# A two-layer decoder on one core: pair 10 of both feed-forward layers by half-size products, halves of the down projection one pair later, the next pair's first remainders ahead of evictions, and 23 warming matmuls

## The chip, the core and the metric

The kernel runs on one core of one Trainium2 chip. The metric is the device time of one execution in microseconds; three runs of the kernel before are shown, with their median.

## The reference, cut to what matters

The program is a decoder trunk with one RG-LRU layer and one RWKV-7 layer, each followed by a gated convolutional feed-forward layer. There are 512 tokens, a width of 1024 and a hidden width of 3072, all in float32. The change lies in the feed-forward layers and in the very first instructions.

```
def _conv_ffn(x, norm, w_up, conv_w, conv_b, w_down):
    h = _rmsnorm(x, norm)
    u = jnp.einsum('btd,df->btf', h, w_up)
    gate = _causal_dwconv(u[..., :D_FF], conv_w, conv_b)
    hid = jax.nn.gelu(gate, approximate=True) * u[..., D_FF:]
    return jnp.einsum('btf,fd->btd', hid, w_down)
```

## The kernel before

Every float32 operand is split into a high part, rounded by a cast, and a low part, the remainder (hi and lo; wh and wl for weights that go through `split`). A product is three matmuls: high by high, high by low, low by high (`mm3`, L77; all its matmuls are recorded at L81). ScalarE (ACT) casts the high parts, VectorE (DVE) subtracts for the low parts. An instruction that waits for the remainder therefore waits for a chain of a load, a cast and a subtraction.

**A feed-forward layer** (`ffn`, L580) treats the 3072 gate columns and the 3072 up columns in 12 pairs of 256 columns each, numbered 0 to 11. A pair's work on TensorE (PE) has one of two forms.

- `Whole` (L696) has four products G0, U0, G1, U1: each is half of the contraction for the gate or the up columns, 24 matmuls of 128x128 by 128x512.
- `Halves` (L725) writes the pair's product as seven half-size products in the manner of Strassen and Winograd, numbered 1 to 7 and made in the order 1, 2, 6, 5, 7 and then 3, 4. Each has 24 matmuls of 128x128 by 128x256. They accumulate into the banks A, D, A, F, A, F, A. `HALVES` says which pairs have this form: 3 to 9 and 11.

For each half-size product, `Halves.weights` makes the weights: some are blocks of the weights as loaded, some are sums of two (on DVE, L736, or by an accumulating transfer on GpSimd's queue, L753 and L206). Then a cast on ACT makes hi and a subtraction on DVE makes lo (both L743). hi1 and lo1 are those of product 1, and so on.

`Halves.product` runs a product and then evicts its bank: ACT copies bank A for products 1, 6 and 7 (L770, tile s); DVE adds bank D to s for 2 (L775), bank F for 7 and 3 (L780, L783), and writes the gate rows gpad (L781, L787). After product 4, `gate` (L681) runs the causal convolution (first tap on ACT, L687; two more on DVE, L689; tile cv) and the gelu on ACT (L690, tile ge), once for each of the pair's two blocks. Then two halves s of the up columns are multiplied by ge (L792, each by both blocks' gelus), cast to the high part of hid on ACT (L793), and the low part is subtracted on DVE (L794).

**The down projection** (`down`, L837) takes hid of two pairs (four blocks of 128) into one half of the output columns: 48 matmuls in two pieces, c0 and c1. The function `between` runs between the pieces: there products 3 and 4 of the current pair are made. So on PE one steady pair runs 1, 2, 6, 5, 7, c0, 3, 4, c1, and then the next pair's 1. The accumulators are added to the residual x on DVE (L871) in the first layer; in the second they go to xtok (L862). The last eight blocks (pairs 8 to 11) are a final projection in two groups of output columns.

**Order.** A tile scheduler keeps, on each engine, an order of its own making; `behind` adds an edge between two instructions for the order alone. The weights are loaded by SyncE's queue in the order of a plan (`plan_weights`, L135), which `gu` and `dd` write: `gu(n)` the blocks of a pair, `dd` those of a down half. `weights_load` and `weights_split` run ahead of use by counts; `cap` and `ahead` limit how far the next pair's weights are made. Raw, high and low blocks of weights share 24 buffers of 0.5 MB.

**The start.** While the first loads are on their way, 17 transposes of the identity run on PE (`WARM`, L382), before the first projection of the RG-LRU layer (L251, then L81).

Of the kernel before, what the change touches and what calls it, by code (L numbers as in the profile page):

```python
# [10 lines left out]
ALU = mybir.AluOpType  # L11
# [14 lines left out]
GN_EPS = 64e-5  # L26
DECAY_C = 0.6065306597126334
N4 = 24
WARM = 17

HALVES = (3, 4, 5, 6, 7, 8, 9, 11)

PARAMS = [
    [("lru_b_in", 16), ("lru_conv_w", 32), ("lru_conv_b", 8),
# [37 lines left out]
class Kernel:  # L72
# [62 lines left out]
    def plan_weights(self):  # L135
# [17 lines left out]
        def ffn(l):  # L153
            up, dn = ("ffn_w_up", (l,)), ("ffn_w_down", (l,))

            def gu(n):
                self.quads[l, n] = len(plan)
                a = lambda i, j: piece(up, j * 512, (1 - i) * DFF + n * 256, 4)
                if n in HALVES:
                    for first, more in (((1, 1), (1, 0)), ((0, 0), None), ((0, 1), None), ((1, 0), (0, 0)), ((1, 1), None)):  # L160
                        plan.append((a(*first), 4, True, more and a(*more)))
                else:
                    for i, j in ((1, 0), (0, 0), (1, 1), (0, 1)):
                        plan.append((a(i, j), 4, False, None))

            def dd(row, n, groups):
                for g in groups:
                    for k in range(0, n, 2):
                        add(dn, row + k * P, g * 512)

            for n in range(12):
                gu(n)
                if 2 <= n < 10:
                    dd((n // 2 - 1) * 512, 4, (n % 2,))
            dd(2048, 8, (0, 1))

        full(("lru_w_in", (0,)), [2, 3, 0, 1])
# [402 lines left out]
    def ffn(self, l, xs, finish, after=None):  # L580
        nc, tc = self.nc, self.tc
        last = l == 1
        with tc.tile_pool(name=f"ffn{l}", bufs=1) as pool:
# [38 lines left out]
            H = T // 2  # L622
# [34 lines left out]
            def behind(ins, prev):  # L657
                tc.add_manual_dep(ins.ins, prev.ins.name, NOSYNC, reason="order")

            def hidden(n):  # L660

                if last and n // 2 % 2:
                    if n == 2:
                        self.drain()
                    if n % 2 == 0:
# [59 lines left out]
            class Halves(Pair):  # L725
# [29 lines left out]
                def product(pair, p):  # L755
# [24 lines left out]
                        tt(s[7], s[7], bank["F"], ALU.add)  # L780
                        stt(gp[:, :, 2 + H :], s[7], -1.0, rb(H, T), ALU.mult, ALU.mult)  # L781
                    if p == 3:
                        tt(s[6], s[6], bank["F"], ALU.add)  # L783
                        if not last:
                            tt(s[6], s[6], rb(H, T), ALU.mult)
                    if p == 4:
                        stt(gp[:, :, 2 : 2 + H], bank["A"], -1.0, rb(0, H), ALU.mult, ALU.mult)  # L787
                        for e in range(2):
                            pair.gate(e)
                        pair.room()  # L790
                        for x, h in ((s[1], lo), (s[6], hi)):
                            tt(x, x, pair.ge[:, :, h], ALU.mult)  # L792
                            nc.scalar.copy(pair.hid[:, :, 0, h], x)  # L793
                            tt(pair.hid[:, :, 1, h], x, pair.hid[:, :, 0, h].bitcast(F32), ALU.subtract)  # L794
# [16 lines left out]
            def products(upto, more=2):  # L811

                while True:
# [1 line left out]
                    at[0] += 1  # L815
                    ahead(at[0] + more)
                    pairs[n].product(p)
                    if p == "G0" and n == 10:
                        self.weights_load(quads[n + 1] + 4)
                    if p == "G1" and n == 2:  # L820
                        self.weights_load(quads[n + 1] + 2)
                    if n == 0 and p in ("G0", "U0"):
                        start(int(p == "U0"))
                    if n == 1 and p == "U0":
# [12 lines left out]
            def down(g, b0, blocks, between=None):  # L837
# [29 lines left out]
                else:  # L867
# [8 lines left out]
                        if between and c == 0:  # L876
                            between()

                    self.project(hids, ev, kb=blocks, join=1 if between else 2, rate=0.5 if final else 2, after=hook, x0=b0)

            rooms = []

# [5 lines left out]
            cap[0] = seq.index((2, "U1")) + 1  # L888
            products((2, "U1"))
            cap[0] = len(seq)  # L890

            def between():
                self.weights_load(quads[3] + 4)
                ahead(at[0] + 1)

            down(0, 0, 4, between)
            ahead(at[0] + 2)
            for n in (*range(3, 10), 11):
                if n == 11:
                    products((10, "U1"))  # L900
                cap[0] = seq.index((n, 7)) + 1
                products((n, 7))
                cap[0] = seq.index((n, 4)) + 1
                ahead(at[0] + 2)
                following = n + 1 in HALVES
                if following:
                    self.weights_load(quads[n + 1] + 2)

                def between():
                    products((n, 3))  # L910
                    cap[0] = len(seq)
                    if following:
                        self.weights_load(quads[n + 1] + 4)
                    products((n, 4))
                    if following:
# [931 lines left out]
```

## Time and profile before

| | us |
|---|---|
| median of three runs | 1282.51 |
| lowest and highest run | 1281.61, 1282.84 |
| the profiled execution, its time | 1282.94 |
| the profiled execution, its span on the core | 1281.2 |
| TensorE busy in the span | 1248.3 |
| VectorE busy | 963.6 |
| ScalarE busy | 654.9 |
| GpSimd busy | 124.0 |

The profiled execution is one run, recorded by the hardware; its time is a little longer than its span, as the work around the first and last instruction belongs to it. The mean granted clock of TensorE in it is 0.994 of full. The page's groups name line, engine, operation and tiles, with the number of instructions, busy time and mean duration. A timeline gives the start in us from the span's start, the duration, and in brackets the idle time before an instruction and what ended it. The chain of waits goes back from the last instruction to what released it, step by step.

### The profile page before, as it was taken

How to read it: one execution, taken by the hardware profiler on the slowest of the kernel's cores; microseconds unless marked ns; L12 is line 12 of the kernel's file. 1: busy time of each engine (PE TensorE's matmuls, PEld its weight loads, DVE VectorE, ACT ScalarE, POOL GpSimd, SP SyncE). 2: the span in 40 equal slices, each digit the busy share in tenths (PEclk: the TensorE clock that was granted, in tenths of full speed). 3: DMA queues.
4: the chain of work that ended last, by engine and by line, in shares of the span. 5: the costliest groups of instructions: out<-in, count | busy, mean ns of one | idle time of the engine just before them, and what ended most of it. 6: DMA issues, size and time to landing. Idle time of an engine off the chain costs nothing.

```text
span 1281.2 us, 23259 instructions
## 1 busy us (share of the span) xinstructions
PE 1248.3 (97%) x9645; PEld 1076.6 (84%) x9645; DVE 963.6 (75%) x1451; ACT 654.9 (51%) x1013; POOL 124.0 (10%) x204
## 2 busy tenths in 40 slices
PE   9999999999999999999999999999999999999997
PEld 7777888999999988877678888778889999999886
DVE  6988688477777777789999877778863767777764
ACT  6697454344444444459845356545742444444442
POOL 0000000000000000010002244410000000000000
PEclk9999999999999999999999999999999999999999
DMA  6322234566666642423203112123345666665431
GB/s 255 99 66 83 92 106 115 148 166 171 174 165 165 197 104 82 140 58 126 82 18 107 44 54 84 61 84 99 117 92 147 168 168 165 164 167 190 105 116 66
DMA packets 46506, 154.08 MB, mean 120 GB/s; under 512 B 5984, under 2 KB 8288, under 8 KB 46272
## 3 DMA queue, kind: packets, MB, share of 16 engines
q1 hardware_dynamic: 38480, 125.32, 30.0%
q0 software_dynamic: 7056, 25.69, 11.6%
q8 instruction: 76, 1.25, 0.4%
q10 hardware_dynamic: 864, 1.57, 0.4%
q14 instruction: 30, 0.25, 0.1%
HBM read 148.05 MB, written 4.52 MB: 119 GB/s over the span
## 4 chain that ended last, share of the span: by engine, by line
PE 35%; DVE 12%; ACT 3%; issue 2%; POOL 1%; POOLq 0%; DVEq 0%; ACTq 0%
PE accA L81 5%; PE acc L81 4%; PE accF L81 4%; PE accU L81 3%; PE accG L81 3%; PE acc L857 3%; PE acc L859 3%; PE acc L858 3%; DVE X L1346 1%; DVE lo L743 1%; DVE wl L127 1%; PE accD L81 1%; DVE DA L1344 1%; DVE cv L689 1%; PE s L1460 1%
## 5 line engine op out<-in xcount | busy, mean ns | idle before, releaser
L127 DVE TENSOR_TENSOR wl<-raw,wh 128x1024 fp32r<-128x1024 f32 (+1 forms) x137 | 164.8, 1213 | 26.0 <-ACT wh L123 24.8
L743 DVE TENSOR_TENSOR lo<-raw,hi 128x1024 fp32r<-128x1024 f32 x112 | 134.7, 1219 | 15.5 <-ACT hi L743 15.4
L123 ACT CAST wh<-raw 128x1024 fp32r<-128x1024 f32 (+1 forms) x136 | 139.2, 1044 | 8.8 <-DMA raw<-in_weights_dram 5.0
L743 ACT CAST hi<-raw 128x1024 fp32r<-128x1024 f32 x112 | 113.5, 1050 | 40.4 <-DVE raw L736 19.3
L81 PE MATMUL accA<-xt,hi 128*128 128x256 f32 x768 | 133.9, 277 | 0.0
L81 PE MATMUL acc<-hid,wh 128*128 128x512 f32 x384 | 118.4, 393 | 1.9 <-ACT wh L123 1.9
L81 PEld LDWEIGHTS accA<-xt,hi 128*128 128x128 f32 x768 | 116.2, 188 | 0.0
L81 PE MATMUL accA<-xt,lo 128*128 128x256 f32 x384 | 106.3, 277 | 0.0
L770 ACT COPY s<-accA 128x512 f32<-128x512 f32 x48 | 28.1, 585 | 136.5 <-PE accA L81 136.5
L687 ACT ACTIVATE cv<-gpad,pv 128x512 f32<-128x512 f32 x48 | 37.5, 812 | 110.3 <-DVE gpad L787 97.5
L81 PEld LDWEIGHTS acc<-hid,wh 128*128 128x128 f32 x384 | 71.3, 190 | 16.2 <-ACT wh L123 2.4
L81 PE MATMUL accU<-xs,wh 128*128 128x512 f32 x256 | 79.5, 392 | 0.0
L81 PE MATMUL accG<-xs,wh 128*128 128x512 f32 x256 | 79.5, 392 | 0.0
L81 PE MATMUL acc<-xs,wh 128*128 128x512 f32 x248 | 77.8, 394 | 0.0
L857 PE MATMUL acc<-wh,hid 128*128 128x512 f32 (+1 forms) x200 | 76.8, 384 | 0.0
L858 PE MATMUL acc<-wh,hid 128*128 128x512 f32 (+1 forms) x200 | 76.8, 384 | 0.0
L859 PE MATMUL acc<-wl,hid 128*128 128x512 f32 (+1 forms) x200 | 76.7, 384 | 0.0
L81 PE MATMUL acc<-hid,wl 128*128 128x512 f32 x192 | 74.2, 394 | 0.0
L689 DVE SCALAR_TENSOR_TENSOR cv<-gpad,pv,cv 128x512 f32<-128x512 f32 x96 | 67.7, 746 | 7.4 <-ACT cv L687 7.3
L81 PEld LDWEIGHTS accA<-xt,lo 128*128 128x128 f32 x384 | 72.2, 188 | 0.0
L206 POOL DMA_DIRECT2D raw<-in_weights_dram x32 | 28.3, 884 | 358.0 <-DVE s L780 131.5
L81 PE MATMUL acc<-mix,wh 128*128 128x512 f32 x192 | 60.6, 399 | 2.2 <-ACT wh L123 2.2
(379 smaller groups left out, 3156.0 us busy)
## 6 DMA issues: line engine op xcount, KB each, us to landing
raw<-in_weights_dram SPq DMA_DIRECT2D x215, 512.0 KB, 3.7
raw<-in_weights_dram POOLq DMA_DIRECT2D x48, 512.0 KB, 5.6
xd<-x SPq DMA_DIRECT2D x8, 256.0 KB, 2.2
AR<-xd SPq DMA_DIRECT2D x1, 2048.0 KB, 9.3
x<-in_xT_dram SPq DMA_DIRECT2D x3, 512.0 KB, 6.9
out_dram<-xtok ACTq DMA_DIRECT2D x4, 256.0 KB, 2.1
out_dram<-xtok SPq DMA_DIRECT2D x4, 256.0 KB, 2.0
raw<-in_weights_dram SPq DMA_DIRECT2D x2, 256.0 KB, 4.9
```

The costliest lines, as they stand in the source:

```text
L81: mm = lambda *a, **kw: self.nc.tensor.matmul(ps, *a, skip_group_check=more, **kw)
L123: put = (self.nc.vector.tensor_copy if dve else self.nc.scalar.copy)(hi, src)
L127: rest = self.nc.vector.tensor_tensor(lo, src, hi.bitcast(F32), ALU.subtract)
L206: self.nc.gpsimd.dma_start(raw, more, accum_op=ALU.add)
L687: nc.scalar.activation(cv, pair.gp[:, e, 0:T], AF.Identity, bias=self.vec(f"ffn_conv_b{l}", fb), scale=cw(0))
L689: nc.vector.scalar_tensor_tensor(cv, pair.gp[:, e, j : j + T], cw(j), cv, ALU.mult, ALU.add)
L743: pair.at[p] = nc.scalar.copy(hi, f[p]), tt(lo, f[p], hi.bitcast(F32), ALU.subtract)
L770: copied = nc.scalar.copy(s[p], bank["A"])
L857: nc.tensor.matmul(ps, hh[:, s], wh[:, k, m], start=kk == 0, stop=False)
L858: nc.tensor.matmul(ps, hl[:, s], wh[:, k, m], start=False, stop=False)
L859: nc.tensor.matmul(ps, hh[:, s], wl[:, k, m], start=False, stop=kk == blocks - 1)
L1344: nc.vector.tensor_tensor(w, A[:, s + 1 :, s : s + 1].to_broadcast([P, n, j]), X[:, s : s + 1, 0:j].to_broadcast([P, n, j]), ALU.mult)
```

## The change

1. `WARM` is 23 and not 17.
2. `HALVES` is 3 to 11 without a gap: pair 10 is made by half-size products too, in both layers.
3. The down halves come one pair later. Before, the halves of pairs 0 and 1 were run after pairs 2 and 3 and so on to pair 9; now after pairs 3 and 4 and so on to pair 10. The plan of loads moves with them. The second layer's tile for hid of pairs 2 and 3 of each four is allocated once.
4. `later` adds two edges: the next pair's low part of product 1 stands ahead of the eviction of product 3 (L783, now L786), and that of product 2 ahead of the eviction of product 4 (L787, now L790). `cap` is lifted before product 3 and not after it, so these weights are made in time for the edges.
5. The final projection of the first layer splits weights three pieces ahead and not two.

Below L660 the lines of the changed kernel are 3 more at first (L783 is L786), and 1 more in `down` (L871 is L872).

```diff
-WARM = 17
+WARM = 23
-HALVES = (3, 4, 5, 6, 7, 8, 9, 11)
+HALVES = range(3, 12)
...
-                if 2 <= n < 10:
-                    dd((n // 2 - 1) * 512, 4, (n % 2,))
+                if 3 <= n < 11:
+                    dd((n - 3) // 2 * 512, 4, ((n - 3) % 2,))
...
+            def later(ins, n, p):
+                if n in pairs and p in pairs[n].at:
+                    behind(ins, pairs[n].at[p][1])
...
                     if p == 3:
-                        tt(s[6], s[6], bank["F"], ALU.add)
+                        later(tt(s[6], s[6], bank["F"], ALU.add), pair.n + 1, 1)
...
                     if p == 4:
-                        stt(gp[:, :, 2 : 2 + H], bank["A"], -1.0, rb(0, H), ALU.mult, ALU.mult)
+                        later(stt(gp[:, :, 2 : 2 + H], bank["A"], -1.0, rb(0, H), ALU.mult, ALU.mult), pair.n + 1, 2)
...
-                    if p == "G0" and n == 10:
+                    if p == "G0" and n == 2:
                         self.weights_load(quads[n + 1] + 4)
-                    if p == "G1" and n == 2:
-                        self.weights_load(quads[n + 1] + 2)
...
-                    self.project(hids, ev, kb=blocks, join=1 if between else 2, rate=0.5 if final else 2, after=hook, x0=b0)
+                    self.project(hids, ev, kb=blocks, join=1 if between else 2, rate=0.5 if final else 2, after=hook, x0=b0, ahead=3 if final else 2)
...
-            for n in (*range(3, 10), 11):
-                if n == 11:
-                    products((10, "U1"))
+            for n in range(3, 12):
                 cap[0] = seq.index((n, 7)) + 1
                 products((n, 7))
                 cap[0] = seq.index((n, 4)) + 1
                 ahead(at[0] + 2)
...
                 def between():
-                    products((n, 3))
                     cap[0] = len(seq)
-                    if following:
+                    if n < 11:
                         self.weights_load(quads[n + 1] + 4)
                     products((n, 4))
...
                 if n < 11:
-                    down(n % 2, (n // 2 - 1) * 4, 4, between)
+                    down((n - 3) % 2, (n - 3) // 2 * 4, 4, between)
```

How the instructions stand now is shown at three places. Buffer numbers are kept in the names.

**VectorE, first layer, from one steady pair's end into the next pair.** lo1 and lo2 are the next pair's remainders of products 1 and 2, gpad the eviction of product 4, cv the convolution, s the up columns. Before:

```order
L783 TENSOR_TENSOR s_3003<-s_3003,accF_3005 128x512
L785 TENSOR_TENSOR s_3003<-s_3003,rb_1450 128x512
L787 SCALAR_TENSOR_TENSOR gpad0_1364<-accA_2915,rb_1450 128x2x256
L743 TENSOR_TENSOR lo1_3143<-raw67_3081,hi1_3142 128x1024
L743 TENSOR_TENSOR lo2_3147<-raw68_3137,hi2_3146 128x1024
L689 SCALAR_TENSOR_TENSOR cv_3176<-gpad0_1364,pv_79,cv_3176 128x512
L689 SCALAR_TENSOR_TENSOR cv_3181<-gpad0_1364,pv_79,cv_3181 128x512
...
L736 TENSOR_TENSOR raw67_3081<-raw66_3078,raw67_3081 128x1024
L792 TENSOR_TENSOR s_2940<-s_2940,ge_3175 128x512
L792 TENSOR_TENSOR s_3003<-s_3003,ge_3175 128x512
L743 TENSOR_TENSOR lo6_3195<-raw67_3081,hi6_3194 128x1024
```

After, in the same place:

```order
L746 TENSOR_TENSOR lo1_3055<-raw65_3019,hi1_3054 128x1024
L786 TENSOR_TENSOR s_2941<-s_2941,accF_2943 128x512
L746 TENSOR_TENSOR lo2_3085<-raw66_3049,hi2_3084 128x1024
L788 TENSOR_TENSOR s_2941<-s_2941,rb_1456 128x512
L790 SCALAR_TENSOR_TENSOR gpad0_1370<-accA_2853,rb_1456 128x2x256
L739 TENSOR_TENSOR raw65_3019<-raw64_3016,raw65_3019 128x1024
L692 SCALAR_TENSOR_TENSOR cv_3114<-gpad0_1370,pv_79,cv_3114 128x512
L692 SCALAR_TENSOR_TENSOR cv_3119<-gpad0_1370,pv_79,cv_3119 128x512
...
L746 TENSOR_TENSOR lo6_3133<-raw65_3019,hi6_3132 128x1024
L795 TENSOR_TENSOR s_2878<-s_2878,ge_3113 128x512
L795 TENSOR_TENSOR s_2941<-s_2941,ge_3113 128x512
```

lo1 and lo2 stood behind gpad and now stand ahead of the evictions of products 3 and 4; the sum of weights (raw65) now comes before the convolution and lo6 before the multiplications of s by ge.

**ScalarE, first layer, at the same place.** ge are the two gelus, COPY of accA the eviction of product 1 of the next pair, hi6 and hi5 casts of its weights. Before:

```order
L687 ACTIVATE cv_3176<-gpad0_1364,pv_79 128x512
L687 ACTIVATE cv_3181<-gpad0_1364,pv_79 128x512
L690 ACTIVATE ge_3175<-cv_3176 128x512
L690 ACTIVATE ge_3175<-cv_3181 128x512
L743 CAST hi6_3194<-raw67_3081 128x1024
L793 CAST hid_3186<-s_2940 128x2x256
L793 CAST hid_3186<-s_3003 128x2x256
L770 COPY s_3252<-accA_3227 128x512
L743 CAST hi5_3254<-raw66_3078 128x1024
```

After:

```order
L690 ACTIVATE cv_3114<-gpad0_1370,pv_79 128x512
L690 ACTIVATE cv_3119<-gpad0_1370,pv_79 128x512
L746 CAST hi6_3132<-raw65_3019 128x1024
L693 ACTIVATE ge_3113<-cv_3114 128x512
L773 COPY s_3190<-accA_3165 128x512
L693 ACTIVATE ge_3113<-cv_3119 128x512
L746 CAST hi5_3192<-raw64_3016 128x1024
L796 CAST hid_3124<-s_2878 128x2x256
L796 CAST hid_3124<-s_2941 128x2x256
L773 COPY s_3253<-accA_3165 128x512
```

The cast hi6 and the copy of accA (product 1) now stand ahead of the second gelu, and hi5 ahead of the casts of hid. Seven of the eight transitions from one halved pair to the next in the first layer have this order.

**ScalarE, second layer, at the same place of a steady pair, after:**

```order
L690 ACTIVATE cv_10942<-gpad1_9475,pv_79 128x512
L690 ACTIVATE cv_10947<-gpad1_9475,pv_79 128x512
L746 CAST hi6_10960<-raw171_10848 128x1024
L693 ACTIVATE ge_10941<-cv_10942 128x512
L746 CAST hi5_11020<-raw170_10845 128x1024
L693 ACTIVATE ge_10941<-cv_10947 128x512
L773 COPY s_11018<-accA_10993 128x512
L796 CAST hid_10952<-s_10708 128x2x256
L796 CAST hid_10952<-s_10770 128x2x256
```

Here hi6 and hi5 stand ahead of a gelu each, and the copy stands behind both gelus; before, both layers had the order that the first of ScalarE's pieces above shows.

More of the change, by code (lines that the diff above doesn't have):

```diff
@@ L664, in hidden @@
                         self.drain()
-                    if n % 2 == 0:
                         self.xhid = self.const.tile([P, 2, 2, 2, T], F32R, tag="x", name="hid", bufs=1)
@@ L886, in room @@
                 return rooms[-1][:, b % 2, 0], rooms[-1][:, b % 2, 1]
-            cap[0] = seq.index((2, "U1")) + 1
             products((2, "U1"))
[L890 to L897, printed above, removed]
-            for n in (*range(3, 10), 11):
-                if n == 11:
-                    products((10, "U1"))
+            for n in range(3, 12):
                 cap[0] = seq.index((n, 7)) + 1
@@ L904, in ffn @@
                 ahead(at[0] + 2)
-                following = n + 1 in HALVES
-                if following:
+                if n < 11:
                     self.weights_load(quads[n + 1] + 2)
                 def between():
-                    products((n, 3))
                     cap[0] = len(seq)
-                    if following:
+                    if n < 11:
                         self.weights_load(quads[n + 1] + 4)
                     products((n, 4))
-                    if following:
+                    if n < 11:
                         ahead(at[0] + 3)
```

## Prediction

> **What bounds the kernel now.** I read the page first, then the waits of TensorE, then the chain of work that ended last, then timelines of the two feed-forward layers. The page says that there is little besides TensorE.
>
> ```profile
> span 1281.2 us, 23259 instructions
> PE 1248.3 (97%) x9645; PEld 1076.6 (84%) x9645; DVE 963.6 (75%) x1451; ACT 654.9 (51%) x1013; POOL 124.0 (10%) x204
> ```
>
> So a change has to take matmul time away, or close some of the 33 us in which TensorE (PE) stood. The waits name who made it stand; three of them lie where this change works.
>
> ```profile
> PE acc L81 <- ACT wh L123: 4.1, 2, 2.2
> PE accF L81 <- DVE lo L743: 4.0, 7, 0.7
> PE acc L251 <- ACT xs L326: 1.2, 1, 1.2
> ```
>
> The second is product 5 of a halved pair (bank F), which waits for VectorE's low part of its own weights, seven times. The chain shows what the two kinds of pairs cost when nothing waits. Columns: start, duration, engine, tile, line, count. First pair 10 of the second layer, a Whole pair (first and last of its four products), then pair 11 by halves, in the order of products 1, 2, 6, 5, 7 and then 3, 4.
>
> ```profile
> 1188.72 5.45 PE accG L81 x24
> ...
> 1205.05 5.44 PE accU L81 x24
> 1210.49 2.87 PE accA L81 x24
> 1213.36 2.88 PE accD L81 x24
> 1216.24 2.74 PE accA L81 x24
> 1218.98 2.72 PE accF L81 x24
> 1221.70 2.72 PE accA L81 x24
> ...
> 1229.88 2.87 PE accF L81 x24
> 1232.75 2.74 PE accA L81 x24
> ```
>
> A Whole pair takes 1210.49 - 1188.72 = 21.77 us, a halved one 2.87 + 2.88 + 2.74 + 2.72 + 2.72 + 2.87 + 2.74 = 19.54 us. The difference, 2.23 us, is what halving is worth if its products never wait.
>
> They do wait. In the timeline of PE below (start, duration, tile, count, idle before and its releaser) are one transition of the first layer in full and the wait in another, then three of the four of the second layer.
>
> ```profile
> 391.61 0.40 PE L81 MATMUL accD<-xs,hi 128*128 128x256 f32 x2
> 397.23 0.39 PE L81 MATMUL accF<-xt,hi 128*128 128x256 f32 x2
> 398.09 0.39 PE L81 MATMUL accF<-xt,lo 128*128 128x256 f32 x1 [0.47 <-DVE lo L743]
> 400.70 0.39 PE L81 MATMUL accA<-xt,hi 128*128 128x256 f32 x2
> 429.30 0.39 PE L81 MATMUL accF<-xt,lo 128*128 128x256 f32 x1 [0.47 <-DVE lo L743]
> 1071.41 0.38 PE L81 MATMUL accF<-xt,lo 128*128 128x256 f32 x1 [0.58 <-DVE lo L743]
> 1102.86 0.39 PE L81 MATMUL accF<-xt,lo 128*128 128x256 f32 x1 [0.71 <-DVE lo L743]
> 1166.35 0.38 PE L81 MATMUL accF<-xt,lo 128*128 128x256 f32 x1 [0.58 <-DVE lo L743]
> ```
>
> Product 5 begins with two matmuls of the high part at 397.23 and then stands. From its first matmul to product 7's (400.70) are 3.47 us against the 2.72 above: 0.75 lost, the idle 0.47 plus 0.28 of refilling. What VectorE (DVE) does before that, and ScalarE (ACT) beside it, in the same transition:
>
> ```profile
> 384.77 2.35 DVE L743 TENSOR_TENSOR lo<-raw,hi 128x1024 fp32r<-128x1024 f32 x2
> 387.04 2.73 DVE L689 SCALAR_TENSOR_TENSOR cv<-gpad,pv,cv 128x512 f32<-128x512 f32 x4
> 390.82 1.29 DVE L792 TENSOR_TENSOR s<-s,ge 128x512 f32<-128x512 f32 x2
> 393.22 1.29 DVE L794 TENSOR_TENSOR hid<-s,hid 128x512 fp32r<-128x512 f32 x2
> 394.43 2.47 DVE L871 TENSOR_TENSOR x<-x,acc 128x512 f32<-128x512 f32 x4
> 396.82 1.22 DVE L743 TENSOR_TENSOR lo<-raw,hi 128x1024 fp32r<-128x1024 f32 x1
> ```
>
> ```profile
> 389.14 1.29 ACT L690 ACTIVATE ge<-cv 128x512 f32<-128x512 f32 x2 [2.73 <-DVE cv L689]
> 392.99 0.58 ACT L770 COPY s<-accA 128x512 f32<-128x512 f32 x1
> 397.43 0.59 ACT L770 COPY s<-accA 128x512 f32<-128x512 f32 x1 [1.97 <-PE accA L81]
> ```
>
> DVE is busy without a gap from the eviction of product 4 to the last low part (396.82), which is product 5's. The first two low parts (2.35 us) are those of the next pair's products 1 and 2. In ACT's rows both gelus stand ahead of the copy of product 1 (392.99).
>
> **Part 1: pair 10 by halves, in both layers.** 2 x 2.23 = 4.5 us less of matmuls. The cover is that its sums, splits and evictions lie on DVE and ACT, which have time (75% and 51%); what is late next is product 5, counted below. Two more accumulating transfers stand on POOL's queue and the loads of pair 10 on SP's; I take these at nothing, since POOL's steady pairs before it do the same in the same room, with 1 us above as bound. Of the rest of the plan (a down half one pair later) the matmuls are the same in number, so it costs nothing by itself.
>
> **Part 2: the remainders ahead of evictions, second layer.** The low parts of products 1 and 2 go ahead of the two evictions, into time in which DVE stands waiting for product 3 and 4. That takes 2.35 us out of the chain to product 5's low part. ACT's new order there gives part of it back: two casts of next weights stand ahead of gelus, some 1 us. What is left, 1.3 us, is more than the longest wait of 0.71. The four waits (0.58, 0.71, 0.71, 0.58; each with 0.28 of refill) go: -3.7 us. If ACT's order took all of it back, 0; if the casts cost nothing, no more than 3.7.
>
> **Part 3: the same in the first layer, where the new order of ACT speaks against it.** In seven of the eight transitions there ACT's order puts the second gelu behind the copy of the next pair's product 1, which waits for that product on PE. Before, it stood ahead of it. Each multiplication by the gelu (L792, now L795) needs the gelus of both blocks, so VectorE's end of the pair begins only then. From the end of product 1 (391.61 in the rows above): 0.20 until a copy starts (the row at 397.43 starts so long after product 6's end at 397.23), 0.48 copy (0.58 to 0.59 with its overlap), 0.65 second gelu (half of 1.29), 0.03 to DVE, 1.26 the two products with the gelu, 0.6 one x, 1.21 two hid, 1.8 three x (of 2.47 for four), 1.22 the low part, 0.05 to PE: 7.5 us, so PE's third matmul of product 5 comes at 399.11 and not 398.09. That is 1.02 later than now, so product 5 loses 0.75 + 1.02 = 1.78 us. Seven times: 12.5. Now three transitions lose 0.75 (366.86 is the third, like the two quoted): 2.3. The difference is +10.2 us. Bounds: if the copy's place costs nothing, the three waits go (-2.3); if the gelu is later still by the refill and each of eight pays it, 8 x 2.1 - 2.3 = +14.5. I take +10.2, since the orders of the engines are fixed in the program and all the durations are rows of this stage.
>
> The table at the head of the Trainium skill's page "TensorE: Matmul & The Clock Gate" calls ScalarE's and VectorE's queues strict FIFOs of 8, and TensorE's one with a partial reorder window. By that rule the gelu cannot pass the copy, and the trace agrees as far as it goes: the copy at 397.43 stands 1.97 us, and nothing passes it.
>
> **Part 4: 23 warming matmuls.** The start, on PE:
>
> ```profile
> 1.44 3.89 PE L382 MATMUL warm<-ident 128*128 128x128 f32 x17 [1.44 <-POOL ident masks.py:199]
> 6.57 2.08 PE L251 MATMUL acc<-xs,wh 128*128 128x512 f32 x4 [1.24 <-ACT xs L326]
> 8.44 1.91 PE L251 MATMUL acc<-xs,wl 128*128 128x512 f32 x4
> 10.15 1.22 PE L251 MATMUL acc<-xs,wh 128*128 128x512 f32 x4
> 11.20 0.62 PE L81 MATMUL acc<-xs,wh 128*128 128x512 f32 x2
> ```
>
> One takes 3.89 / 17 = 0.229, so 23 end at 6.71: 0.14 after the first data now, and the gap of 1.24 is closed. The first eight matmuls take 0.45 to 0.5 each, later ones 0.23: full pace came some 3.6 us after unbroken work began at 6.57. With work unbroken from 1.44 it would be there at 6.71, and 12 matmuls at 0.227 end at 9.4, not 11.20: -1.8. If pace does not come earlier, +0.1. I take -1.7.
>
> The same page, in its section on the HAM clock gate (Part 1), says that the clock is let to full after about 3.4 us of sustained work, in windows that run free of the kernel. The rows agree in the 3.6 us; by the rule's free windows the gain would lie between -1.0 and -1.8 by estimate.
>
> **Part 5: the end of the first layer.** The last down projection, now split one step further ahead (L123, L127):
>
> ```profile
> 511.26 2.18 PE L81 MATMUL acc<-hid,wh 128*128 128x512 f32 x6 [1.94 <-ACT wh L123]
> 515.38 0.72 PE L81 MATMUL acc<-hid,wh 128*128 128x512 f32 x2
> 518.45 1.07 PE L81 MATMUL acc<-hid,wh 128*128 128x512 f32 x4
> ```
>
> The wait of 1.94 goes, since the cast it waited for now stands between the casts of hid. With it may go the slow stretch behind it: 11 matmuls from 511.26 to 515.38 took 4.1 us where 0.227 each would be 2.5, so 1.6. Together -3.5. But the first cast of the second group now stands on ACT behind three scaled blocks of x, each of which needs a finished column block of the group before: about 2 us from the end of the first group (518.45 in the rows) until PE can go on, and half a chance of the slow stretch again. -3.5 + 2.0 + 0.8 = -0.7; bounds -3.5 and +1.
>
> **Sum**, against the profiled execution's 1282.94 (span 1281.2, and 1.7 around it): -4.5 - 3.7 + 10.2 - 1.7 - 0.7 = -0.4, so 1282.5. That execution lies 0.43 above the median of the runs, 1282.51, so the forecast on the median's footing is 1282.1.
>
> **The rivals.**
>
> Rival B, faster: the second gelu costs nothing, as VectorE has other work until then or the copy comes in time. For it: DVE is busy to the last in the rows above, and idle of an engine off the path is free. Against it: the sum of 7.5 us from product 1 has only fixed steps in it. Time: -4.5 - 3.7 - 2.3 - 1.7 - 0.7 = -12.9, so 1269.6 after the same 0.43. Whether product 5 in the first layer takes 2.7 us decides.
>
> Rival C, slower: the seven new gaps bring half pace. After the idle of 1.94 at 511.26 PE ran at half pace for 4.1 us, at a price of 1.6, and the granted clock of that stretch shows it:
>
> ```profile
> 480.00:520.00 40.00, 38.02 (x213) 32.57 (x213) 28.47 (x37) 17.66 (x23) 0.00 (x0) 0.96 0.33 92
> ```
>
> After the waits of 0.71 nothing of the kind followed. The new gap, 0.47 + 1.02 = 1.5 us, lies between. If 1.5 us suffices each time, 7 x 1.6 = 11.2 come on top: 1293.3. It decides at a gap between 0.71 and 1.94; if it depends on where the gap falls, some of the seven pay, and the time lies from 1284 upwards. The section on the clock gate says that half pace comes back only after an idle window of about 3.4 us. By that rule rival C would not happen, and the forecast would stand; the trace differs, as 1.94 sufficed, so the measurement decides.
>
> **How the numbers follow.** Forecast 0.68, rival B 0.16, rival C 0.16. The forecast's own range is 1278 to 1286: the end of the layer (-2.8 to +1.7 about its value), the start (+1.8) and the size of the new wait (7 x 0.3 either way). A measurement of this kernel can tell about 0.2% from no change, 2.6 us: faster is under 1279.9, slower over 1285.1. Of the forecast 0.15 lies under it and 0.07 over it; with all of B and C that makes faster 0.31, slower 0.23, same 0.46. The range 1270 to 1289 takes in the forecast, half of B and half of C.
>
> **What would show it.** In the changed kernel: pair 10 takes 19.5 us on PE and not 21.8; product 5 in the second layer 2.72 without idle; in the first layer seven waits of about 1.5 us of bank F for DVE's low part, with ACT's second gelu right behind a copy that waited for bank A; PE at full pace before 7 us, L81 starting near 9.5. Wrong would be: first-layer products 5 of 2.7 to 3.0 us (then B), or matmuls of 0.45 us behind those waits and granted clocks under 1.00 between 240 and 480 us (then C), or product 5 still waiting in the second layer, which would leave out the 3.7.

## The result, and the profile after

The changed kernel takes 1290.37 us (median of 7 runs, 1285.73 to 1291.79), the kernel before 1282.67 (7 runs, 1281.61 to 1283.84). The ratio is 1.0052, with a 95% interval of 1.0036 to 1.0068: slower by about half a per cent, where no change was forecast as likeliest. The medians lie 7.7 us apart and the ratio gives 6.7; below both are given where they differ. The times of the changed kernel's runs go with the mean granted clock on record for each: it is 0.997 in the fastest run and 0.989 in the two slowest. The profiled execution of the changed kernel took 1288.59, with a span of 1286.8.

The page of the changed kernel has the same shape as before: TensorE (PE) busy 97% of the span, but for 2.5 us less than before in a span that is 5.6 us longer.

```profile
span 1286.8 us, 23651 instructions
PE 1245.8 (97%) x9795; PEld 1081.3 (84%) x9795; DVE 974.0 (76%) x1465; ACT 661.3 (51%) x1025; POOL 130.2 (10%) x210
```

Its waits on PE name the places. Columns as before: waited for, us in total, times, longest.

```profile
PE accF L81 <- DVE lo L746: 9.9, 7, 1.4
PE l2a L1125 <- ACT l2h L123: 3.7, 1, 3.7
PE acc L81 <- ACT wh L123: 3.7, 2, 2.1
...
PE acc L81 <- ACT hid L796: 1.5, 1, 1.5
```

Product 5 (accF) waited 4.0 us in seven places before, and now 9.9 in seven. The second row had 1.2 us before and was no part of the forecast: l2h are the second weights of the RWKV layer's low-rank products, which come after the first feed-forward layer.

**The start** came as written. 23 transposes end where the first projection begins, its 12 matmuls run at full pace, and L81 begins at 9.48 and not 11.20.

```profile
1.44 5.14 PE L382 MATMUL warm<-ident 128*128 128x128 f32 x23 [1.44 <-POOL ident masks.py:199]
6.63 1.19 PE L251 MATMUL acc<-xs,wh 128*128 128x512 f32 x4
...
9.48 0.61 PE L81 MATMUL acc<-xs,wh 128*128 128x512 f32 x2
```

**One transition of the first layer**, the fourth of the seven that wait. First ScalarE (ACT), then VectorE (DVE), then PE; the bracket is the idle time before and what ended it.

```profile
377.92 0.64 ACT L693 ACTIVATE ge<-cv 128x512 f32<-128x512 f32 x1 [0.65 <-DVE cv L692]
381.72 0.59 ACT L773 COPY s<-accA 128x512 f32<-128x512 f32 x1 [3.17 <-PE accA L81]
382.20 0.64 ACT L693 ACTIVATE ge<-cv 128x512 f32<-128x512 f32 x1
```

```profile
378.47 1.21 DVE L746 TENSOR_TENSOR lo<-raw,hi 128x1024 fp32r<-128x1024 f32 x1
382.87 1.29 DVE L795 TENSOR_TENSOR s<-s,ge 128x512 f32<-128x512 f32 x2 [3.19 <-ACT ge L693]
...
387.68 1.22 DVE L746 TENSOR_TENSOR lo<-raw,hi 128x1024 fp32r<-128x1024 f32 x1
```

```profile
381.52 0.40 PE L81 MATMUL accD<-xs,hi 128*128 128x256 f32 x2
...
387.14 0.39 PE L81 MATMUL accF<-xt,hi 128*128 128x256 f32 x2
388.95 0.39 PE L81 MATMUL accF<-xt,lo 128*128 128x256 f32 x1 [1.42 <-DVE lo L746]
...
391.57 0.39 PE L81 MATMUL accA<-xt,hi 128*128 128x256 f32 x2
```

ACT stands 3.17 us before the copy of product 1, whose end on PE is the start of product 2 (381.52), and the second gelu runs right behind it. DVE, with all else done, stands 3.19 us for that gelu and then works through to product 5's low part. From the end of product 1 to PE's next matmul of product 5 are 388.95 - 381.52 = 7.43 us (forecast 7.5), and product 5 takes 391.57 - 387.14 = 4.43 us (forecast 4.50).

**The second layer** has no such wait left; in the chain of waits, product 5 (accF) of a transition follows product 6 without a break:

```profile
1098.63 2.74 PE accA L81 x24
1101.37 2.72 PE accF L81 x24
```

**The end of the first layer and what comes next**, on PE: the final projection's two waits and its last matmul, the sum of squares (ssq) and the broadcast (rbc) of the next normalisation, and the first matmul with l2h.

```profile
514.44 1.84 PE L81 MATMUL acc<-hid,wh 128*128 128x512 f32 x5 [1.53 <-ACT hid L796]
...
522.68 1.89 PE L81 MATMUL acc<-hid,wh 128*128 128x512 f32 x7 [2.07 <-ACT wh L123]
...
549.53 0.39 PE L81 MATMUL acc<-hid,wl 128*128 128x512 f32 x1
549.76 5.30 PE L81 MATMUL lwa<-hx,wa 128*128 128x512 f32 x22
...
556.02 0.95 PE L349 MATMUL ssq<-inv_d,sqacc 128*128 128x1 f32 x8
...
558.41 1.21 PE L361 MATMUL rbc<-ident,rs 128*128 128x128 f32 x8 [1.10 <-POOL rs L357]
...
591.08 0.79 PE L1125 MATMUL l2a<-ta,l2h 128*128 128x512 f32 x1 [3.69 <-ACT l2h L123]
```

In the kernel before, the same stage reads:

```profile
543.22 0.39 PE L81 MATMUL acc<-hid,wl 128*128 128x512 f32 x1
...
549.10 1.16 PE L361 MATMUL rbc<-ident,rs 128*128 128x128 f32 x8 [0.87 <-POOL rs L357]
550.01 4.67 PE L81 MATMUL lwa<-hx,wa 128*128 128x512 f32 x19
...
582.25 0.50 PE L1137 MATMUL l2a<-ta,l2h 128*128 128x512 f32 x1 [1.22 <-ACT l2h L123]
```

lwa are the first of the low-rank products; they need nothing from the normalisation. Before, 19 of the 48 ran behind the broadcast, 4.5 us of work under the chain that leads from it over the mixes to l2h. Now all of them stand ahead of it. They fill PE there, but what holds the broadcast back stands on DVE: it adds the projection's last four accumulators to x, and the normalisation waits for the squares of these four blocks. Before:

```profile
535.48 0.69 DVE L871 TENSOR_TENSOR x<-x,acc 128x512 f32<-128x512 f32 x1 [2.86 <-PE acc L81]
...
538.23 0.68 DVE L871 TENSOR_TENSOR x<-x,acc 128x512 f32<-128x512 f32 x1
...
540.98 0.68 DVE L871 TENSOR_TENSOR x<-x,acc 128x512 f32<-128x512 f32 x1
...
543.72 0.68 DVE L871 TENSOR_TENSOR x<-x,acc 128x512 f32<-128x512 f32 x1
```

After, with the end of the last squares (sqacc):

```profile
545.65 0.69 DVE L872 TENSOR_TENSOR x<-x,acc 128x512 f32<-128x512 f32 x1 [9.89 <-PE acc L81]
546.56 0.69 DVE L872 TENSOR_TENSOR x<-x,acc 128x512 f32<-128x512 f32 x1 [0.22 <-PE acc L81]
...
547.82 0.68 DVE L872 TENSOR_TENSOR x<-x,acc 128x512 f32<-128x512 f32 x1
...
552.69 0.68 DVE L872 TENSOR_TENSOR x<-x,acc 128x512 f32<-128x512 f32 x1
...
555.08 0.68 DVE L342 TENSOR_TENSOR sqacc<-sqacc,sq 128x512 f32<-128x512 f32 x1
```

Before, a block came every 2.75 us, and when the projection's last matmul had begun (543.22), DVE took the last block 0.5 us later. Now the blocks come bunched: DVE has no gap from 546.56 to the end of the last squares, and takes the fourth block 3.16 us after the last matmul began (549.53), behind work for the first three. So the broadcast starts 8.88 us after that matmul and not 5.88. From the broadcast to the first matmul with l2h are 33.15 us before and 32.67 after: the chain has much the same length in both, though PE has 4.5 us less work under it, so the broadcast's delay is handed on.

The granted clock (the figure after POOL's count) shows half pace, in which matmuls take about twice as long: 0.96 is one stretch of it in 40 us. Where the seven waits lie it is 1.00; behind the broadcast and the wait of 3.69 it is 0.88.

```profile
280.00:320.00 40.00, 38.58 (x275) 36.08 (x274) 28.10 (x37) 18.13 (x25) 3.51 (x4) 1.00 0.62 160
...
560.00:600.00 40.00, 36.31 (x141) 28.31 (x140) 38.09 (x71) 29.53 (x44) 3.71 (x17) 0.88 0.20 69
```

The starts of the same instruction in both timelines tell where the time went:

| place on PE | before | after | after - before |
|---|---|---|---|
| first product of the first feed-forward layer | 157.34 | 154.08 | -3.3 |
| second piece after product 4 of pair 11 | 497.93 | 502.54 | +4.6 |
| last matmul of the final projection | 543.22 | 549.53 | +6.3 |
| broadcast of the next normalisation | 549.10 | 558.41 | +9.3 |
| first matmul with l2h | 582.25 | 591.08 | +8.8 |
| first product of the second feed-forward layer | 888.03 | 898.85 | +10.8 |
| end of the span | 1281.2 | 1286.8 | +5.6 |

So the first layer lost 7.9 us up to the end of pair 11's products, the stage behind it another 6.2, and the second layer won 5.2. The 6.2 are 1.7 in the final projection, 3.0 from its last matmul to the broadcast, -0.5 in the chain to l2h, and 2.0 behind that, with the half pace there.

### The profile page after: what moved, and what is told of

It reads as the page before. It is cut to its first block, busy times and chain, and to the rows that moved or that the text cites. A ratio compares the mean times of both kernels' runs of the same rounds, so it can differ in the third digit from the quotient of the medians.

```text
span 1286.8 us, 23651 instructions
## 1 busy us (share of the span) xinstructions
PE 1245.8 (97%) x9795; PEld 1081.3 (84%) x9795; DVE 974.0 (76%) x1465; ACT 661.3 (51%) x1025; POOL 130.2 (10%) x210
## 4 chain that ended last, share of the span: by engine, by line
PE 42%; DVE 6%; ACT 3%; issue 2%; POOLq 0%; POOL 0%; ACTq 0%; DVEq 0%
PE accA L81 8%; PE acc L81 4%; PE accF L81 4%; PE acc L858 3%; PE acc L859 3%; PE acc L860 3%; PE accU L81 3%; PE accG L81 3%; PE accD L81 2%; DVE X L1334 1%; PE s L1448 1%; PE acc L1280 1%; DVE wl L127 1%; PE acc L1281 1%; PE pd L1530 1%
## 5 line engine op out<-in xcount | busy, mean ns | idle before, releaser
L127 DVE TENSOR_TENSOR wl<-raw,wh 128x1024 fp32r<-128x1024 f32 (+1 forms) x129 | 155.2, 1210 | 20.3 <-ACT wh L123 19.6
L746 DVE TENSOR_TENSOR lo<-raw,hi 128x1024 fp32r<-128x1024 f32 x126 | 150.8, 1218 | 19.7 <-ACT hi L746 14.8
L81 PE MATMUL accA<-xt,hi 128*128 128x256 f32 x864 | 150.7, 277 | 0.0
L746 ACT CAST hi<-raw 128x1024 fp32r<-128x1024 f32 x126 | 128.3, 1047 | 19.0 <-PE acc L859 6.5
L123 ACT CAST wh<-raw 128x1024 fp32r<-128x1024 f32 (+1 forms) x128 | 131.2, 1043 | 7.3 <-DMA raw<-in_weights_dram 3.8
L81 PEld LDWEIGHTS accA<-xt,hi 128*128 128x128 f32 x864 | 130.7, 188 | 0.0
L81 PE MATMUL acc<-hid,wh 128*128 128x512 f32 x384 | 118.0, 391 | 3.7 <-ACT wh L123 2.1
L81 PE MATMUL accA<-xt,lo 128*128 128x256 f32 x432 | 120.2, 278 | 0.0
L81 PEld LDWEIGHTS acc<-hid,wh 128*128 128x128 f32 x384 | 70.0, 188 | 18.1 <-ACT wh L123 2.5
L81 PEld LDWEIGHTS accA<-xt,lo 128*128 128x128 f32 x432 | 81.1, 188 | 0.9
L81 PE MATMUL acc<-xs,wh 128*128 128x512 f32 x248 | 78.9, 399 | 0.0
L81 PE MATMUL acc<-hid,wl 128*128 128x512 f32 x192 | 73.6, 389 | 0.0
L81 PE MATMUL acc<-mix,wh 128*128 128x512 f32 x192 | 60.5, 397 | 1.6 <-ACT wh L123 1.6
L81 PE MATMUL accU<-xs,wh 128*128 128x512 f32 x192 | 59.8, 392 | 0.0
L81 PE MATMUL accG<-xs,wh 128*128 128x512 f32 x192 | 59.8, 392 | 0.0
```

Source lines behind the costliest of these rows:

```text
L81: mm = lambda *a, **kw: self.nc.tensor.matmul(ps, *a, skip_group_check=more, **kw)
L123: put = (self.nc.vector.tensor_copy if dve else self.nc.scalar.copy)(hi, src)
L127: rest = self.nc.vector.tensor_tensor(lo, src, hi.bitcast(F32), ALU.subtract)
L746: pair.at[p] = nc.scalar.copy(hi, f[p]), tt(lo, f[p], hi.bitcast(F32), ALU.subtract)
```

## The experiments

Each run beside the kernel before on the same chip; the ratio is to that kernel. The kernel before took 1281.4 to 1282.6 in these comparisons.

**One edge more: the copy behind the second gelu.** The edit, in the changed kernel:

```diff
-                    nc.scalar.activation(pair.ge[:, e], cv, AF.Gelu_apprx_tanh)
+                    pair.gelu = nc.scalar.activation(pair.ge[:, e], cv, AF.Gelu_apprx_tanh)
...
                             behind(copied, pair.at[6][0])
+                            behind(copied, pairs[pair.n - 1].gelu)
```

> The changed kernel with one more edge of order: ScalarE's copy of a pair's product 1 stands behind the second gelu of the pair before it. Theory (the copy's place makes the seven waits): the seven idle times of 1.42 us before product 5 in the first layer go, each with 0.29 of refill, 7 x 1.71 = 12.0 us, so 1290.4 - 12.0 = 1278.4, and TensorE shows no wait for bank F in that layer. Rival (VectorE's own work ahead of the low part is what is late, and the gelu only stands where it would have waited anyway): idle of 0.5 to 1.4 stays, and the time is 1283 to 1290.

Measured: 1278.98 us, ratio 0.9975 (0.9966 to 0.9984). No wait for bank F is left in either layer; the first of PE's waits is now that of l2h.

```profile
PE l2a L1126 <- ACT l2h L123: 3.7, 1, 3.7
```

That is 11.4 us less than the changed kernel by the medians and 9.9 by the ratios, where 12.0 was expected. The rows say why it is less: product 2 of one pair and of the next start 32.18 us apart in the changed kernel (381.52 and 413.70) and 30.70 here (378.38 and 409.08), not 30.45 as between two early pairs of the kernel before (238.25 and 268.70). One edge of order on ACT takes all seven waits away, so the copy's place made them; the rival falls.

**The final projection split two pieces ahead.** In the changed kernel:

```diff
-... x0=b0, ahead=3 if final else 2)
+... x0=b0, ahead=2)
```

> The changed kernel with the final projection of the first layer split two pieces ahead again, not three. Theory (splitting three ahead moves the 20 matmuls of the RWKV layer's first low-rank product from behind the normalisation's broadcast to ahead of it, so nothing covers the chain from there to the second low-rank weights): the distance from the start of that broadcast to the first matmul with these weights stays at about 32 us, but begins 4.6 us earlier; the wait of 3.69 shrinks to about 1.2 and the half-pace stretch behind it goes: 1290.4 - 4.2 - 2 = about 1284. Rival (the final projection's own waits cost as much as they gave): the two waits of 1.53 and 2.07 become one of 1.94 with half pace behind it (1.6), nothing else changes: 1290 within 1.

Measured: 1282.46 us, ratio 1.0008 (1.0000 to 1.0017), 7.9 us less than the changed kernel by the medians, 5.6 by the ratios. The seven waits stay and the wait for l2h is back at 1.2:

```profile
PE accF L81 <- DVE lo L746: 10.0, 7, 1.4
...
PE l2a L1125 <- ACT l2h L123: 1.2, 1, 1.2
```

At this place 19 low-rank matmuls stand behind the broadcast again, the last four blocks come every 2.75 us, and the broadcast starts 5.89 us after the projection's last matmul, as in the kernel before. So the second loss hangs on this one argument. Some 6 us were expected.

**Both edits together.**

> Both edits of the two runs before it. Theory (two separate causes): the gains add, 1290.4 - 12.0 - 6 = 1272 us, about 10 under the kernel before. Rival (one cause, the later stage only swallowed time that the first layer lost): no better than the better of the two alone, 1278.

Measured: 1274.04 us, ratio 0.9937 (0.9923 to 0.9950). By the ratios the two gains add: 9.9 + 5.6 would be 15.5, and 14.7 is measured (by the medians 11.4 + 7.9 and 16.3). So they are two causes, and the rival of one cause falls.

**Without the two edges for the remainders.**

```diff
-                        later(tt(s[6], s[6], bank["F"], ALU.add), pair.n + 1, 1)
+                        tt(s[6], s[6], bank["F"], ALU.add)
...
-                        later(stt(gp[:, :, 2 : 2 + H], bank["A"], -1.0, rb(0, H), ALU.mult, ALU.mult), pair.n + 1, 2)
+                        stt(gp[:, :, 2 : 2 + H], bank["A"], -1.0, rb(0, H), ALU.mult, ALU.mult)
```

> The changed kernel without the two edges that put the next pair's remainders ahead of evictions. Theory (these edges remove the waits in the second layer and cause the order of ScalarE that lengthens them in the first): product 5 waits again in both layers as in the kernel before, by about 0.47 in the first (7 x 0.76 = 5.3 in place of 12.0) and 0.58 to 0.71 in the second (six of about 0.9 in place of none, 5.6): 1290.4 - 6.7 + 5.6 = 1289. Rival (the edges are without effect, the order of ScalarE comes from the down halves' new place): the seven waits of 1.42 stay, 1290 or more.

Measured: 1286.42 us, ratio 1.0038 (1.0026 to 1.0051), 4.0 us less than the changed kernel by the medians and 1.8 by the ratios, whose intervals overlap.

```profile
PE accF L81 <- DVE lo L746: 6.2, 11, 0.7
```

Product 5 waits eleven times, five in the first layer by 0.47 to 0.48 and six in the second by 0.58 to 0.72. The expectation had seven in the first; with five of 0.76 it would have been 1287.8. Without the edges both gelus stand ahead of the copy on ACT again, and the waits of 1.42 are gone; so the edges cause these, through ACT's order, and they remove the second layer's waits. Both halves of that are shown.

**The kernel before with the final projection split three pieces ahead.**

```diff
-... x0=b0)
+... x0=b0, ahead=3 if final else 2)
```

> The kernel before with one edit: the final projection of the first layer is split three pieces ahead. Theory (this argument alone moves the low-rank product's matmuls ahead of the normalisation and costs what the changed kernel lost after the first layer): slower by 4 to 8 us, 1286 to 1290, and the wait for the second low-rank weights grows from 1.2 to 3.7. Rival (the loss there needs the halved pair 10 or the later down halves): within 1 us of the kernel before.

Measured: 1286.89 us, ratio 1.0037 (1.0025 to 1.0049): 4.3 us slower by the medians and 4.7 by the ratio, inside the theory's range. The broadcast, 8.88 us after the projection's last matmul, and the wait are those of the changed kernel:

```profile
551.85 1.16 PE L361 MATMUL rbc<-ident,rs 128*128 128x128 f32 x8 [1.10 <-POOL rs L357]
584.50 0.79 PE L1137 MATMUL l2a<-ta,l2h 128*128 128x512 f32 x1 [3.69 <-ACT l2h L123]
```

The argument alone does it, without the halved pair 10.

**The kernel before with 23 warming matmuls.** The edit is `WARM = 23`.

> The kernel before with 23 warming matmuls and nothing else. Theory (the gap before the first projection closes and full pace comes 3.6 us after unbroken work began): the first matmul of L81 starts near 9.5 in place of 11.2, and 1.7 us are won, 1280.4. Rival (what is won at the start is waited for again later, since later loads and the chain at the end of the RG-LRU layer do not move): within 0.5 of the kernel before.

Measured: 1280.72 us, ratio 0.9989 (0.9980 to 0.9997); L81 begins at 9.25.

1.8 us are won by the medians (0.4 to 2.6 by the interval), as forecast, and nothing takes them back.

**Pair 10 by halves and the later down halves alone.** The changed kernel with 17 warming matmuls, two pieces ahead and no edges (the three edits above, undone together).

> The changed kernel with 17 warming matmuls, without the two edges of order and with the final projection split two ahead: what is left is pair 10 by halves and the down halves one pair later. Theory (halving is worth 2.23 a layer, but each further transition between halved pairs brings a further wait of product 5): -4.5, and five waits of 0.76 for three and a half in the first layer (+1.2), six of 0.9 for four in the second (+1.8): -1.5, 1280.5. Rival (the waits are hidden by the down halves' new place): -4.5, 1277.5.

Measured: 1282.06 us, ratio 0.9993 (0.9983 to 1.0002), between 1277.95 and 1283.73 in 12 runs. The eleven waits are there. Halving pair 10 without the edges is worth some 0.5 us by the median, and the interval takes in nothing and the 1.5 expected; the rival's 4.5 it does not take in. In the profiled execution the first layer, to the end of pair 11's products, is 0.4 us longer than before, and the second 1.2 shorter.

**Best so far: fewer low-rank steps in the final projection.** The changed kernel with the edge of the first experiment, two pieces ahead, and the background work of the final projection at half the rate (the rate says how many steps of other work, here the low-rank weights' scaling and splitting, go between two pieces of the projection):

```diff
-... rate=0.5 if final else 2, after=hook, x0=b0, ahead=3 if final else 2)
+... rate=0.25 if final else 2, after=hook, x0=b0, ahead=2)
```

> The changed kernel with the copy behind the second gelu, the final projection split two ahead, and its background work at a rate of 0.25 and not 0.5, which leaves 24 of the 48 low-rank matmuls behind the normalisation's broadcast where 19 were. Theory (that chain has a fixed length of about 32 us, and what covers it saves TensorE time): the wait of 1.24 for the second low-rank weights goes, 1274.0 - 1.2 = 1272.8. Rival (another wait of the stage takes its place): 1274 within 0.5.

Measured: 1264.10 us, ratio 0.9861 (0.9848 to 0.9873): 10 us under the run with both edits, where 1.2 was expected. Behind the broadcast stand 24 low-rank matmuls, and the wait for l2h is gone:

```profile
537.46 1.16 PE L361 MATMUL rbc<-ident,rs 128*128 128x128 f32 x8
538.37 5.84 PE L81 MATMUL lwa<-hx,wa 128*128 128x512 f32 x24
...
568.31 0.39 PE L1126 MATMUL l2a<-ta,l2h 128*128 128x512 f32 x1
```

The chain was not of a fixed length here, as the theory had it: from the broadcast to the first l2a matmul are 30.85 us, and ACT, in another order, begins the last cast of l2h 29.44 us behind the broadcast, where it was 32.06 in the run with both edits. So this run does not show that the further matmuls made the wait go. All waits of the final projection went too, and so the theory missed most of the gain. The next run asks for it.

**The same rate in the kernel before.** The edit is `rate=0.25` in place of 0.5.

> The kernel before with one edit: the background work of the first layer's final projection at a rate of 0.25. Theory (the rate alone takes the low-rank weights' casts out of ScalarE's way at the layer's end, so the waits of 0.9, 1.94 and 1.22 there go with their half-pace stretches, and two half-pace stretches of 1.7): 1282.6 - 4 - 1.2 - 3 = about 1274.5, some 8 us. Rival (the gain of the run before needs the change's halved pair 10 there): under 2 us, 1281.

Measured: 1274.23 us, ratio 0.9945 (0.9931 to 0.9958): 7.2 us faster than the kernel before. PE stands nowhere from 480 to 520 us, and the granted clock, 0.96 there and from 640 to 680 before, is 1.00 in both.

```profile
480.00:520.00 40.00, 40.00 (x230) 34.96 (x230) 31.54 (x43) 20.90 (x28) 0.00 (x0) 1.00 0.43 131
...
640.00:680.00 40.00, 40.00 (x198) 31.51 (x197) 39.66 (x87) 12.87 (x23) 4.79 (x15) 1.00 0.23 73
```

The rate acts by itself. In ACT's order at the layer's end, casts of the low-rank weights stand among those of the projection's own; fewer of them there is the likely reason, which no run varied alone.

**The best kernel without the edges for the remainders (and the gelu).**

> The best kernel so far (1264.1) without the two edges of order for the next pair's remainders and without the edge for the second gelu. Theory (the edges are worth the waits of product 5 that they remove: five of about 0.77 in the first layer, six of about 0.92 in the second): 1264.1 + 3.9 + 5.5 = 1273.5. Rival (in this order of the layer's end the waits would be made up for later): 1264 to 1267.

Measured: 1271.24 us, ratio 0.9920 (0.9906 to 0.9933), 7.1 us more than the best (7.6 by the ratios, since the kernel before took 1.15 less in this comparison). The eleven waits are back:

```profile
PE accF L81 <- DVE lo L746: 6.2, 11, 0.7
```

6.2 us of idle and 11 x 0.28 of refill would be 9.3; 7.1 came out. Here too a pair of the best kernel takes 0.2 to 0.6 us more than the 30.45 of the early pairs without any wait listed, so less is lost.

**The best kernel without the edge for the gelu.**

> The best kernel so far without the edge that keeps the copy of product 1 behind the second gelu. Theory: seven waits of 1.42 with 0.29 of refill come back and nothing else changes: 1264.1 + 12.0 = 1276.1. Rival (gaps of 1.42 bring half pace now and then): more than 1278.

Measured: 1274.95 us, ratio 0.9950 (0.9938 to 0.9963), 10.9 us more than the best (11.4 by the ratios), with the seven waits:

```profile
PE accF L81 <- DVE lo L746: 9.9, 7, 1.4
```

The granted clock is 1.00 in the rows of 280 to 320 and 440 to 480 us here too, so these gaps cost their own length and no half pace. The best kernel and these two runs say the same as the changed kernel and the first and fourth experiments, without the second loss: the edges for the remainders are worth 7 to 8 us if the copy stands behind the gelu, and cost something if it does not: 3.7 here, and in the changed kernel 4.0 by the medians but 1.8 by the ratios.

## Why the prediction was wrong

The time was forecast at 1282.1, in a range from 1270 to 1289, and is 1290.4. By its own steps:

- **Part 1, pair 10 by halves, -4.5.** The halving itself cannot be read alone from a median; with the waits that it brings it was worth 0.5 (the interval reaches from 2.2 faster to 0.3 slower). In the sum these waits were counted in parts 2 and 3, so nothing contradicts the term: of the 0.4 longer and 1.2 shorter layers of that run, two further waits in each, at the prediction's prices 1.5 and 1.8, leave some -1.1 and -3.0 for the halving, by estimate.
- **Part 2, the second layer's waits, -3.7.** Right. All went, and the second layer as a whole won 5.2 where parts 1 and 2 gave 2.2 + 3.7 = 5.9; a pair there takes 30.7 to 31.0 us, where the early pairs of the kernel before take 30.45.
- **Part 3, the first layer, +10.2.** Right in mechanism, place and number: seven waits of 1.42 in place of 1.5, product 5 at 4.43 in place of 4.50. 7 x 1.71 = 12.0 less the 2.3 of before is +9.7. (0.75 + 1.02 is 1.77, not 1.78; that changes nothing.) The first experiment shows the cause, not only the place.
- **Part 4, the start, -1.7.** Right: 1.72 in the trace, 1.8 by the medians in the run with this part alone.
- **Part 5, the end of the first layer, -0.7, bounds -3.5 and +1.** This is the step that failed. It took the argument "three pieces ahead" as one of casts alone, asked only where PE waits in the final projection, and put all that stands behind the projection at nothing. Its own wait was priced about rightly (2.07 for the second group, forecast as 2.0); a further one of 1.53 for hid was not foreseen, and half pace behind them did not come in this execution. What the runs show in its place is +6.2 by the second layer where -0.7 was forecast. The new order bunches the projection's last blocks, so the broadcast of the next normalisation starts 8.88 us after the projection's last matmul and not 5.88, and the chain behind the broadcast keeps its length but for 0.5. All low-rank matmuls stand ahead of it now, so PE has less to do under this chain, its wait for l2h grew from 1.22 to 3.69, and half pace followed. The 8.88 is the same in all four recorded kernels that split three ahead, and 5.88 or 5.89 stands in all five that split two ahead at the rate of 0.5. The run of the kernel before with this argument alone (+4.7 by the ratio) and that of the changed kernel without it (-5.6) show that the argument is the cause. How the loss divides between the bunched blocks and the moved low-rank matmuls is read from the rows; no run moved one without the other.
- **Rival B, 0.16**, fell with part 3. **Rival C, 0.16**, was on the right side with the wrong mechanism: the seven gaps of 1.42 brought no half pace (granted clock 1.00 in their stretch). What decided lay behind them, at the layer's end.

The terms as they came: -1.7 at the start, -1.5 more by the end of the RG-LRU layer (where one of two waits went; that is luck, since both stand again in the first two experiments, whose kernels are the same up to there), +7.9 in the first layer (+9.7 of waits, -2.2 of halving, the rest, 0.4, not assigned), +6.2 behind it, -5.2 in the second: +5.7, and the spans differ by 5.6. The profiled execution lies 1.8 us under the median of its runs. These spread over 6 us, and the granted clock goes with that, as said above; where their stretches at half pace lie is known of the recorded execution alone.

By the medians, undoing "three ahead" gave 7.9 in the changed kernel and adding it to the kernel before cost 4.3; by the ratios it is 5.6 and 4.7, and the intervals reach over one another. The granted clock explains most of what is left. Its mean over all runs goes from 0.9924 to 0.9956 in the one and from 0.9944 to 0.9930 in the other; span times the share not granted falls by 4.2 us and rises by 1.8, by estimate. Of the mean times' 6.5 and 4.5 that leaves 2.4 and 2.7, beside the 3.0 - 0.5 that the rows show.

What stays open: why the half-pace stretches fall where they do, and what the rate changes at the layer's end, beyond the order that the rows show.

## What to carry to other kernels

Give an edge of order to one engine, and read the new order of every engine: here an edge meant for VectorE let a copy that waits for TensorE pass a gelu on ScalarE, and a gain of 7 us became a loss of 2 to 4. When an edit changes how far ahead work is prepared, read the order of the stage behind it too: here the blocks that the next normalisation waits for came bunched and not one by one, its broadcast started 3.0 us later, the chain that hangs on it handed the delay on, and the matmuls that had filled PE under that chain were already done. The best kernel here keeps the change's edges and its halved pair, and is 18.5 us faster than the kernel before by the medians.

## What the runs showed of the hardware

The same wait is not always followed by half pace. The second wait of the final projection, 2.07 us, was followed by seven matmuls in 1.89 us in the changed kernel (shown above), and in the kernel of the first experiment, by the same seven in 2.83:

```profile
513.60 2.83 PE L81 MATMUL acc<-hid,wh 128*128 128x512 f32 x7 [2.07 <-ACT wh L123]
```

Seven gaps of 1.42 in 195 us brought none. In the granted clock that each trace records, stretches at half pace last 3.413 us or twice that, but for the last, which the end of the record cuts; and in the kernel before the first three start 399.35 and 136.54 us apart, which is 117 and 40 times 3.413. The Trainium skill's page "TensorE: Matmul & The Clock Gate" says in its part 1, on the HAM clock gate, that the gate looks at windows of about 3.4 us that run free of the kernel; what came after the same wait in two executions agrees with that. The same part says that half pace needs about one idle window of that length; here it came after 2.07 us of idle, and after 1.94 in the kernel before, so in this case a shorter gap was enough.
